# Two residual gates of a diffusion layer: column sums by float32r passes of a high and a low part in place of plain float32 products

## The chip, the cores and the metric

The kernel runs on one NeuronCore of one Trainium2 chip. The metric is the device time of one execution in microseconds, as the median of several runs; shorter is better. One more execution was taken with the profiler; the profile and the trace are of that one.

## The reference

One layer over 1024 latent tokens and 256 context tokens of width 1024, cut to what matters here:

```python
m_lat = silu(c) @ w_mod[l] + b_mod[l]
sh1, sc1, g1, sh2, sc2, g2 = split(m_lat, 6)
h_lat = rms_norm(x, norm1_g) * (1 + sc1) + sh1
y_lat = token_mixers(h_lat, h_ctx, ...)      # retention and differential attention
x = x + g1 * y_lat
h2 = rms_norm(x, norm2_g) * (1 + sc2) + sh2
x = x + g2 * conv_ffn(h2, ...)
return rms_norm(x, final_g)
```

The two residual gates g1 and g2 are rows of 1024 numbers, products of the conditioning vector silu(c) with two 1024 x 1024 blocks of w_mod plus a bias. All inputs and outputs are float32.

## The kernel before

The work runs in stages on one core: the modulation of the first norm and the turned input; the combined input projection in seven column blocks of 512 (blocks 2, 5, 6 for the context, 1, 0, 3, 6, 4), each streamed as four slices of weights; retention beside the last of these blocks; differential attention; the output projection; the gated MLP with a seven-product scheme for the up and the down projection; the final norm.

Nearly all products are made in three float32r passes. An operand is split into a high part, a copy rounded to float32r (ScalarE), and a low part, the difference (VectorE). `passes` (lines 128 to 133) then adds high x high, high x low and low x high into one PSUM tile; its three matmuls are lines 131, 132 and 133 of the profile. A few products are plain float32, whose operands are not split; each of them shows as two matmul records.

The change lies in the stage of the input projection from block 5 to block 0. `transposed` (from line 468) makes one tile of 128 x 512 outputs for each head and half of the tokens: eight k, three passes each, and one `tick()` behind each k. Behind the eighth it calls `rotated` (line 440), which turns the tile: ScalarE copies the swapped quarters or halves (L445, tile xb), VectorE multiplies and adds (L448, L449, L450, tile xa). For the attention's keys `split_store` (line 433) then makes a high part (L436) and a low part (L437) in a tile xhl and stores it (L438). For the queries of the retention `decayed` (line 427) instead lets GpSimd make two scaled copies in a tile xq (L430) and stores them (L431). xhl and xq share one ring of two buffers (tag "xhl" in the pool er). `natural` makes token-major tiles, L411 to L425 its endings. Weights come by `slice_load` (L189) into raw and are split by `split_slice` (L196 the high part, L197 the low part).

Beside this stage runs a generator, `modulations` (from line 490). One `next` of it is made at each tick; the stage has 240 ticks, the generator goes through 233 yields. It has 32 steps of seven yields, eight steps for each of four blocks of w_mod: shift, scale and gate of the second norm, and the gate of the first, in the order g1 (i = 0), two shifts and scales, g2 (i = 3). A step loads a 128 x 1024 piece (L497) and adds it, scaled by the column of silu(c), into an accumulator macc (L511); the accumulators start at zero (L506) with the bias in row 0 (L507). What is left is the sum of macc over the 128 partitions, which `modulated2` makes:

```python
if i in (0, 3):
    dst = g1_d if i == 0 else g2_d
    for n in range(2):
        pg = pst.tile([P, 512], F32, name="pg", tag="tr")
        mm(pg, ones, acc[:, n * 512 : (n + 1) * 512], start=True, stop=True)
        st = ev.tile([P, 512], F32, name="st", bufs=3)
        nc.scalar.copy(st, pg)
        nc.sync.dma_start(out=dst[:, n * 512 : (n + 1) * 512], in_=st)
        yield
```

A 128 x 128 matrix of ones times macc gives the sum in every partition (L528, tile pg); ScalarE copies it out (L530) and it is stored (L531) for the output projection and for the down projection, which read it much later. For i = 1 and 2 the sums are made as columns, by products with two columns of ones (L536). These sums begin one step after their last accumulation for i = 0, 1, 2, and behind the last step for i = 3, where they fall on the last head of block 0.

Where nothing else is said, a planner puts the instructions on the engines: from an estimate of durations it takes, for each engine that is free, the ready instruction that stands first in the source. On each engine the order is then fixed. Other parts of the kernel (the start, attention, the first blocks of the up projection, the end) pin the order of the source on chosen engines by `in_order`; this stage does not. `issue_after` in `modulations` keeps each load and each accumulation behind the newest store and rotation.

The matrix ones (line 112) is also read by `spare`, a few products at the start that only keep TensorE busy (line 655), and by L536.

Of the kernel before, what the change touches and what calls it, by code (L numbers as in the profile page):

```python
# [8 lines left out]
F32 = mybir.dt.float32  # L9
F32R = mybir.dt.float32r  # L10
BF16 = mybir.dt.bfloat16
AF = mybir.ActivationFunctionType
ALU = mybir.AluOpType
# [4 lines left out]
P = 128  # L18
# [51 lines left out]
def r32(ap):  # L70
    return ap.bitcast(F32)
# [3 lines left out]
def kernel(  # L75
# [16 lines left out]
    nc = tc.nc  # L92
    mm = nc.tensor.matmul

    kp = ctx.enter_context(tc.tile_pool(name="kp", bufs=1))
# [13 lines left out]
    nc.sync.dma_start(out=ident, in_=consts[:, K_ID : K_ID + P])  # L109
    mhalf = kp.tile([P, 32], F32, name="mhalf")  # L110
    nc.vector.memset(mhalf, -0.5)
    ones = kp.tile([P, P], F32, name="ones")
    nc.vector.memset(ones, 1.0)

    def rsqrt(out_ap, in_ap, mul, eps, n):
# [39 lines left out]
    with ExitStack() as p1:  # L155
# [334 lines left out]
        def modulations():  # L490
# [11 lines left out]
            for n in range(n_steps):  # L502
                i, k = divmod(n, KD)
                if k == 0:
                    maccs[i] = m2p.tile([P, D], F32, name="macc", bufs=2)
                    nc.gpsimd.memset(maccs[i], 0.0)  # L506
                    nc.sync.dma_start(out=maccs[i][0:1, :], in_=rows[:, R_BMOD + (2 + i) * D : R_BMOD + (3 + i) * D])  # L507
                if n + 2 < n_steps:
                    step_load(n + 2)
                with after("dve"):  # L510
                    nc.vector.scalar_tensor_tensor(out=maccs[i], in0=wms.pop(n), scalar=csil[:, k, 0:1], in1=maccs[i], op0=ALU.mult, op1=ALU.add)  # L511
                for _ in range(MOD_TICKS):
                    if done is not None and k > 0:
                        next(done, None)
                    yield
                if k == KD - 1:
                    done = modulated2(i)
# [4 lines left out]
        def modulated2(i):  # L522
            acc = maccs.pop(i)
            if i in (0, 3):
                dst = g1_d if i == 0 else g2_d
                for n in range(2):
                    pg = pst.tile([P, 512], F32, name="pg", tag="tr")
                    mm(pg, ones, acc[:, n * 512 : (n + 1) * 512], start=True, stop=True)  # L528
                    st = ev.tile([P, 512], F32, name="st", bufs=3)
                    nc.scalar.copy(st, pg)  # L530
                    nc.sync.dma_start(out=dst[:, n * 512 : (n + 1) * 512], in_=st)  # L531
                    yield
            else:
                pg = pst.tile([P, KD, 2], F32, name="pg2", tag="tr")
                for d in range(KD):
                    mm(pg[:, d, :], acc[:, d * P : (d + 1) * P], ones[:, 0:2], start=True, stop=True)  # L536
                    yield
                if i == 1:
                    nc.vector.tensor_copy(m2[:, 0, :], pg[:, :, 0])
                else:  # L540
                    nc.vector.tensor_scalar(out=m2[:, 1, :], in0=pg[:, :, 0], scalar1=1.0, scalar2=None, op0=ALU.add)
                    nc.vector.tensor_tensor(out=m2[:, 1, :], in0=m2[:, 1, :], in1=cl[:, COL_N2 : COL_N2 + KD], op=ALU.mult)
# [4 lines left out]
        with ExitStack() as p0:  # L547
# [121 lines left out]
            start = len(nc.cur_bb.bb.instructions)  # L669
# [49 lines left out]
            part = [pool.tile([P, 512], F32, name="pn", tag="mm") for pool in (ps_a, ps_a, ps_b, ps_b)]  # L719
# [48 lines left out]
        er = p1.enter_context(tc.tile_pool(name="er", bufs=2, reuse_waits="tile"))  # L768
# [26 lines left out]
        with tc.tile_pool(name="rc0", bufs=1) as r0:  # L795
# [20 lines left out]
            acc = r0.tile([P, 8], F32, name="acc")  # L816
# [241 lines left out]
        start = len(nc.cur_bb.bb.instructions)  # L1058
# [59 lines left out]
    with ExitStack() as p2:  # L1118
# [4 lines left out]
        start = len(nc.cur_bb.bb.instructions)  # L1123
        order = sorted(TAU.items(), key=lambda it: it[1] % 1.0)
        for n in range(n_units + 8):
# [6 lines left out]
            if n in (8, 10, 12, 14):  # L1132
                a, i = divmod(n // 2 - 4, 2)
# [210 lines left out]
    with ExitStack() as p4:  # L1344
# [142 lines left out]
        start = len(nc.cur_bb.bb.instructions)  # L1487
# [95 lines left out]
    with ExitStack() as p5:  # L1583
# [43 lines left out]
        acc = [fin.tile([P, D], F32, name=f"acc{t}") for t in range(NT)]  # L1627
# [80 lines left out]
        start = len(nc.cur_bb.bb.instructions)  # L1708
# [130 lines left out]
```

## Time and profile before

| what | us |
|---|---|
| median of 3 runs (lowest to highest) | 1388.44 (1387.87 to 1389.47) |
| the profiled execution | 1388.11 |
| its span, first to last instruction | 1386.3 |
| TensorE busy in it | 1365.4 |
| VectorE, ScalarE, GpSimd busy | 1018.0, 738.6, 346.4 |
| the four gate products (eight records of L528) | first at 136.7, last at 264.1 |

In the lists of the profile PE is TensorE (PEld its weight loads, PEldq the queue of those), DVE VectorE, ACT ScalarE, POOL GpSimd and SP SyncE (SPq its queue of transfers). L528 is line 528 of the kernel. A row of a timeline has the start and the duration in microseconds, the engine, the line, the operation with what it writes and reads, how often it stands there in succession (x2), and in brackets how long the engine had been idle and what ended that; "issue" means that nothing in the trace explains it. A row of a source line or a tile has the durations as lowest, median and highest in nanoseconds. A row of waits has the total, how often, and the longest. A row of transfers ends with the microseconds from issue to landing. A row of windows has the stretch, its length, then for PE, PEld, DVE, ACT and POOL the busy time and the number of instructions, the granted clock of TensorE as a share of the full one, the busy share of the DMA engines and GB/s. Matmuls overlap in the array, so that their durations add up to more than the time that they take; the distance of starts is what they cost.

### The profile page before, as it was taken

The numbers are of one execution on the slowest core, as the hardware profiler recorded it, in microseconds if no ns is written. First come the engines' busy times: TensorE is split into PE (matmuls) and PEld (weight loads), VectorE is DVE, ScalarE is ACT, GpSimd is POOL, SyncE is SP. The second block draws the span as 40 slices with busy tenths as digits, with TensorE's granted clock in tenths as the row PEclk, the third lists the DMA queues.
The fourth block names the chain that finished last, engine by engine and source line by source line (L and its number), as shares of the span: only waits on it lengthen the run. The fifth ranks groups of instructions, "written<-read, shape, count | busy, mean of one in ns | idle before, by whom it ended". The sixth has DMA issues, their size and how long they took to land.

```text
span 1386.3 us, 19666 instructions
## 1 busy us (share of the span) xinstructions
PE 1365.4 (98%) x7028; PEld 1145.9 (83%) x7028; DVE 1018.0 (73%) x1512; ACT 738.6 (53%) x1410; POOL 346.4 (25%) x384
## 2 busy tenths in 40 slices
PE   8999999999999999999999999999999999999997
PEld 6788788888888799998888888888888888888886
DVE  5967866623467898896347998887778877898756
ACT  5536534313466789987037654555545555455533
POOL 1310001501446433411101343222332220043003
PEclk9999999999999999999999999999999999999999
DMA  9467887786678488631221223332323326953334
GB/s 384 153 206 252 295 265 249 254 273 185 191 221 231 133 217 186 140 94 70 106 99 46 92 107 114 114 114 92 114 100 113 111 69 224 393 180 109 122 99 152
DMA packets 107305, 231.14 MB, mean 167 GB/s; under 512 B 9604, under 2 KB 42884, under 8 KB 105288
## 3 DMA queue, kind: packets, MB, share of 16 engines
q1 hardware_dynamic: 98936, 204.73, 43.3%
q0 software_dynamic: 8128, 24.91, 7.9%
q8 instruction: 55, 0.90, 0.3%
q14 instruction: 42, 0.34, 0.1%
q10 hardware_dynamic: 144, 0.26, 0.1%
HBM read 165.37 MB, written 64.23 MB: 166 GB/s over the span
## 4 chain that ended last, share of the span: by engine, by line
PE 65%; DVE 1%; POOL 1%; issue 0%; ACT 0%; DMA 0%; SPq 0%; POOLq 0%; ACTq 0%; DVEq 0%
PE chain L131 6%; PE chain L132 6%; PE chain L133 6%; PE c L132 5%; PE c L133 5%; PE c L131 5%; PE pv L929 5%; PE pA L897 5%; PE third L131 3%; PE third L133 3%; PE third L132 3%; PE pt L917 2%; PE po L133 2%; PE po L132 2%; PE po L131 2%; PE second L131 1%
## 5 line engine op out<-in xcount | busy, mean ns | idle before, releaser
L131 PE MATMUL pl<-hT,whi 128*128 128x512 f32 x256 | 107.6, 420 | 0.0
L131 PE MATMUL chain<-T,whi 128*128 128x512 f32 x264 | 102.8, 389 | 0.0
L132 PE MATMUL chain<-T,whi 128*128 128x512 f32 x264 | 102.7, 389 | 0.0
L133 PE MATMUL chain<-T,wlo 128*128 128x512 f32 x264 | 102.7, 389 | 0.0
L133 PE MATMUL pl<-hT,wlo 128*128 128x512 f32 x256 | 100.4, 392 | 0.0
L132 PE MATMUL pl<-hT,whi 128*128 128x512 f32 x256 | 100.3, 392 | 0.0
L900 DVE TENSOR_REDUCE mt<-pA 128x1 f32<-128x1280 f32 x64 | 95.2, 1490 | 3.8 <-PE pA L897 2.3
L133 PE MATMUL c<-whi,ghl 128*128 128x512 f32 x232 | 90.4, 390 | 0.0
L131 PE MATMUL c<-whi,ghl 128*128 128x512 f32 x232 | 90.3, 389 | 0.0
L132 PE MATMUL c<-wlo,ghl 128*128 128x512 f32 x232 | 90.3, 389 | 0.0
L1310 POOL TENSOR_TENSOR cmb<-wrb 128x512 f32<-128x512 f32 x20 | 30.3, 1517 | 237.6 <-DMA wrb<-w_up 157.3
L897 PE MATMUL pA<-ks,qhl 128*128 128x512 f32 (+1 forms) x384 | 89.6, 368 | 0.0
L904 ACT ACTIVATE p<-pA,mt 128x1280 f32<-128x1280 f32 x64 | 85.5, 1336 | 3.8 <-DVE mt L900 3.4
L131 PE MATMUL pn<-whi,hT 128*128 128x512 f32 x192 | 85.0, 443 | 0.0
L445 ACT ACTIVATE xb<-pl 32x512 f32<-32x512 f32 (+1 forms) x88 | 52.0, 591 | 61.6 <-PE pl L133 41.9
L1161 ACT CAST whi<-cmb 128x512 fp32r<-128x512 f32 x62 | 38.4, 622 | 77.5 <-PE chain L132 64.3
L929 PE MATMUL pv<-va,aT 128*128 128x128 f32 x640 | 77.1, 276 | 0.4 <-DVE yT L958 0.3
L897 PEld LDWEIGHTS pA<-ks,qhl 128*128 128x128 f32 x384 | 67.9, 189 | 11.5
L133 PE MATMUL pn<-whi,hT 128*128 128x512 f32 x192 | 75.8, 396 | 1.0 <-POOL hT L610 1.0
L132 PE MATMUL pn<-wlo,hT 128*128 128x512 f32 x192 | 75.4, 393 | 0.0
L929 PEld LDWEIGHTS pv<-va,aT 128*128 128x128 f32 x640 | 74.0, 192 | 1.2 <-DVE yT L958 0.8
L1162 DVE TENSOR_TENSOR wlo<-cmb,whi 128x512 fp32r<-128x512 f32 x62 | 58.7, 951 | 18.1 <-ACT whi L1161 18.1
(336 smaller groups left out, 3889.7 us busy)
## 6 DMA issues: line engine op xcount, KB each, us to landing
raw<-w_in SPq DMA_DIRECT2D x32, 512.0 KB, 6.0
wm<-w_mod SPq DMA_DIRECT2D x32, 512.0 KB, 4.6
wra<-w_up SPq DMA_DIRECT2D x24, 512.0 KB, 3.3
wrb<-w_up SPq DMA_DIRECT2D x23, 512.0 KB, 3.5
W<-w_down SPq DMA_DIRECT2D x44, 256.0 KB, 6.2
ad<-s SPq DMA_DIRECT2D x20, 512.0 KB, 3.4
wra<-ad SPq DMA_DIRECT2D x20, 512.0 KB, 3.3
wrb<-ad SPq DMA_DIRECT2D x18, 512.0 KB, 4.6
```

The source lines that it names most:

```text
L131: mm(ps, lh, rh, start=first, stop=False, skip_group_check=more)
L132: mm(ps, lh, rl, start=False, stop=False, skip_group_check=more)
L133: mm(ps, ll, rh, start=False, stop=last, skip_group_check=more)
L445: nc.scalar.activation(xb[q * blk : (q + 1) * blk, :], pt[o : o + blk, :], AF.Copy, scale=scale)
L897: mm(self.pa[m][:, c0:c1], self.q[:, i, m, qs], self.k[:, m, c0:c1], start=(i == 0), stop=(i == 1))
L900: nc.vector.tensor_reduce(out=self.mt[:, m : m + 1], in_=self.pa[m][:, :LK], axis=AX.X, op=ALU.min)
L904: nc.scalar.activation(self.p[m], self.pa[m][:, :LK], AF.Exp, scale=-1.0, bias=self.mt[:, m : m + 1], accum_out=self.s[:, m : m + 1])
L917: nc.tensor.transpose(self.pt[g][:, i, :], self.p[0][:, (4 * g + i) * P : (4 * g + i + 1) * P], ident)
L929: mm(self.pv, self.aT[:, c, :], self.v[:, c, :], start=(c == 0), stop=(c == NKT - 1))
L1161: nc.scalar.copy(hi, src)
L1162: nc.vector.tensor_tensor(out=lo, in0=src, in1=r32(hi), op=ALU.subtract)
L1310: nc.gpsimd.tensor_tensor(out=s1, in0=b1, in1=b2, op=ALU.add)
```

## The change

The sums of the two gates are made in two float32r passes. ScalarE makes a high part of each half of macc, VectorE a low part, in a tile of the xhl ring; three yields later two matmuls with ones, one for each part, add into the same PSUM tile. The products of ones with the high and the low part together give the sum to nearly float32's precision. The matrix ones is now allocated as float32r and read as plain float32 by the other uses. `modulated2` has four yields for each half in place of one, so the generator goes through 239 of the stage's 240 ticks.

```diff
-    ones = kp.tile([P, P], F32, name="ones")
+    ones_r = kp.tile([P, P], F32R, name="ones")
+    ones = r32(ones_r)
     nc.vector.memset(ones, 1.0)
...
             if i in (0, 3):
                 dst = g1_d if i == 0 else g2_d
                 for n in range(2):
+                    part = acc[:, n * 512 : (n + 1) * 512]
+                    hl = er.tile([P, 2, 512], F32R, name="xhl")
+                    nc.scalar.copy(hl[:, 0, :], part)
+                    nc.vector.tensor_tensor(out=hl[:, 1, :], in0=part, in1=r32(hl[:, 0, :]), op=ALU.subtract)
+                    for _ in range(3):
+                        yield
                     pg = pst.tile([P, 512], F32, name="pg", tag="tr")
-                    mm(pg, ones, acc[:, n * 512 : (n + 1) * 512], start=True, stop=True)
+                    for a in range(2):
+                        mm(pg, ones_r, hl[:, a, :], start=(a == 0), stop=(a == 1))
                     st = ev.tile([P, 512], F32, name="st", bufs=3)
                     nc.scalar.copy(st, pg)
                     nc.sync.dma_start(out=dst[:, n * 512 : (n + 1) * 512], in_=st)
                     yield
```

## The prediction

> **What bounds the kernel.** I read the page first, then the waits of TensorE over the whole span, then the timeline around the four products of the two gates.
>
> ```profile
> span 1386.3 us, 19666 instructions
> ## 1 busy us (share of the span) xinstructions
> PE 1365.4 (98%) x7028; PEld 1145.9 (83%) x7028; DVE 1018.0 (73%) x1512; ACT 738.6 (53%) x1410; POOL 346.4 (25%) x384
> ...
> PEclk9999999999999999999999999999999999999999
> ```
>
> ```profile
> PE pt L917 <- ACT aT L923: 1.9, 3, 0.7
> ```
>
> TensorE is busy for 1365.4 of 1386.3 us at full clock, and the largest entry in the list of its waits is 1.9 us in three pieces. So a microsecond taken out of TensorE's stream comes off the time, unless a later wait takes it back, and one put into it is paid. This profiled execution took 1388.11 us (1.8 more than its span), the median of the three runs is 1388.44; I sum changes and add them to the median. A difference below 0.2%, 2.8 us, is about what a measurement of this kernel cannot tell from no change.
>
> **What the products cost now.** The timeline of TensorE at the first one, and the rows of its source line:
>
> ```profile
> 136.44 0.40 PE L133 MATMUL pl<-hT,wlo 128*128 128x512 f32 x1
> 136.68 1.02 PE L528 MATMUL pg<-macc,ones 128*128 128x512 f32 x2
> 137.14 0.79 PE L131 MATMUL pl<-hT,whi 128*128 128x512 f32 x1
> 137.77 0.39 PE L132 MATMUL pl<-hT,whi 128*128 128x512 f32 x1
> 138.00 0.39 PE L133 MATMUL pl<-hT,wlo 128*128 128x512 f32 x1
> ```
>
> ```profile
> L528 PE MATMUL pg<-macc,ones x8: 590/592/596, 136.7 to 264.1; 128*128 128x512 f32 x8
> L528 PEldq EVENT_SEMAPHORE  x2: 51/948/1846, 132.6 to 258.1; - x2
> ```
>
> Durations overlap, so cost is read from starts. Neighbouring float32r passes start 0.23 us apart (137.77 to 138.00). From L133 at 136.44 to L132 at 137.77 are 1.33 us; with L131 alone between them it would be two spacings, 0.46. One plain product, two records of 592 ns, thus costs the stream 0.87 us. There are four (eight records). Each becomes two float32r passes of the same shape, 0.46 us, which removes 0.41 us each: **1.64 us in all, 0.12%**. That is the most that the arithmetic itself can give, and it is below what can be measured.
>
> [...]
>
> The last row also shows what a wait of a product does: the weight queue took two semaphore waits, 0.05 and 1.85 us long, the first at 132.6, yet the array did not idle before 136.68, because the queue runs some 4 us ahead. A late operand costs only what it is late by when the array arrives. Queued behind it are the pl passes, which cannot go round it.
>
> **First gate: what is added.** Per half, ScalarE copies the sums to a high part and VectorE subtracts, then three ticks (nine passes) later come the products. So the first pair is due 10 spacings after 136.44, at 138.74. ScalarE and VectorE at that time:
>
> ```profile
> 137.53 0.28 ACT L840 ACTIVATE kd<-kd,lg 128x1 f32<-128x1 f32 x1
> 139.33 0.62 ACT L436 CAST xhl<-xa 128x512 fp32r<-128x512 f32 x1 [1.51 <-issue]
> 139.97 1.20 ACT L445 ACTIVATE xb<-pl 32x512 f32<-32x512 f32 x2
> 141.19 0.59 ACT L530 COPY st<-pg 128x512 f32<-128x512 f32 x1
> ```
>
> ```profile
> 137.23 0.69 DVE L448 SCALAR_TENSOR_TENSOR xa<-pl,rtab 128x512 f32<-128x512 f32 x1 [1.66 <-ACT xb L445]
> 137.84 0.68 DVE L449 TENSOR_TENSOR xb<-xb,rtab 128x512 f32<-128x512 f32 x1
> 138.56 0.69 DVE L450 TENSOR_TENSOR xa<-xa,xb 128x512 f32<-128x512 f32 x1
> 139.17 1.28 DVE L511 SCALAR_TENSOR_TENSOR macc<-wm,csil,macc 128x1024 f32<-128x1024 f32 x1
> 140.36 0.68 DVE L437 TENSOR_TENSOR xhl<-xa,xhl 128x512 fp32r<-128x512 f32 x1
> 140.97 1.28 DVE L511 SCALAR_TENSOR_TENSOR macc<-wm,csil,macc 128x1024 f32<-128x1024 f32 x1
> ```
>
> Two things stand here. The prices: a high part is 0.62 us (L436), a low part 0.68 us (L437), the same shapes and types as the new ones. And a lag: the head that ends on TensorE at 136.44 has its L445 only at 139.97, some 3 us later. The next window's rotation is thus still in VectorE's queue when the array comes for the pair. The high part also needs a buffer of the two-deep xhl ring, whose earlier content must have been stored:
>
> ```profile
> 135.00 0.52 SPq L438 DMA_DIRECT2D dk<-xhl  x1
> ```
>
> ```profile
> dk<-xhl SPq DMA_DIRECT2D x1, 512.0 KB, 3.2
> ```
>
> That store is issued at 135.00 and lands at 138.2, so the high part ends at 138.8 at the earliest, in ScalarE's gap between 137.81 and 139.33. The low part then goes where the planner puts it in VectorE's order: in place of the sum at 139.17 it ends at 139.85, behind L437 at 141.65, behind the second sum (which also precedes it in the source) at 142.9. Against 138.74 the array waits **1.1, 2.9 or 4.2 us**; nothing if the planner moves the pair itself further back. It plans with durations of its own, and the lag shows that VectorE runs later than it planned. I take 2.6, about the middle of 1.1 and 4.2, as no row prefers an end. The second half should find its parts in time: four ticks of 0.69 us and the first pair lie between, and TensorE's wait has used up the lag. Net for this gate at TensorE: 2.6 - 2 x 0.41 = +1.8 us.
>
> What takes some of this back is the one place in this stage where TensorE waits already, for weights of the next two blocks:
>
> ```profile
> PE pn L132 <- DVE wlo L197: 0.5, 2, 0.3
> ```
>
> ```profile
> 152.94 1.22 DVE L197 TENSOR_TENSOR wlo<-raw,whi 128x1024 fp32r<-128x1024 f32 x1
> 154.39 0.69 DVE L448 SCALAR_TENSOR_TENSOR xa<-pl,rtab 128x512 f32<-128x512 f32 x1 [0.23 <-ACT xb L445]
> ```
>
> ```profile
> 154.32 0.65 SPq L189 DMA_DIRECT2D raw<-w_in  x1
> ```
>
> ```profile
> 161.78 1.05 ACT L196 CAST whi<-raw 128x1024 fp32r<-128x1024 f32 x1 [3.66 <-DMA raw<-w_in]
> ```
>
> A TensorE that comes 1.8 us later no longer meets this 0.5: +1.3 us remain. But the same place sets a floor. The load at 154.32 waits for the buffer that L197 at 152.94 frees, and ScalarE at 161.78 waits for that load; VectorE has only 0.23 us of slack beside it. Two low parts put 2 x 0.68 = 1.36 us ahead of it, so the weights come some 1.1 us later, even if the products never waited. The larger of the two holds: **+1.3 us**. On ScalarE the two high parts (1.24 us) mostly fill its gaps; if they don't, they push the same chain by at most as much, which the upper end holds. The SyncE queue gets no new transfer; its two gate stores move back by three ticks or so, with weight loads behind them, and those loads are the ones just priced. In the xhl ring two more tiles go round, so the next head's copy waits for a store one generation younger; that is ScalarE's lag again, off TensorE's path until the place above.
>
> **Second gate.** Here ScalarE and VectorE are not late:
>
> ```profile
> 256.92 1.20 ACT L445 ACTIVATE xb<-pl 64x512 f32<-64x512 f32 x2 [4.29 <-issue]
> 262.41 1.20 ACT L445 ACTIVATE xb<-pl 64x512 f32<-64x512 f32 x2 [4.29 <-issue]
> ```
>
> ```profile
> 263.70 0.69 DVE L448 SCALAR_TENSOR_TENSOR xa<-pl,rtab 128x512 f32<-128x512 f32 x1 [3.47 <-ACT xb L445]
> ```
>
> ```profile
> 258.74 0.36 SPq L431 DMA_DIRECT2D rqk<-xq  x1
> ```
>
> ```profile
> rqk<-xq SPq DMA_DIRECT2D x1, 512.0 KB, 2.8
> ```
>
> ```profile
> 262.16 1.03 PE L528 MATMUL pg<-macc,ones 128*128 128x512 f32 x2
> ```
>
> ScalarE idles 4.29 us and VectorE 3.47 us before the head's rotation. The buffer's store lands at 258.74 + 2.8 = 261.5, so the two parts are made by 262.9, ahead of a pair due three ticks (2.1 us) after 262.16. Later xq tiles on GpSimd wait for a younger store, with no TensorE work near behind them. The idle time hides both parts: **-0.82 us**. Without that cover they would cost up to 0.62 + 0.68 per half.
>
> Ones as float32r: the other uses read it as plain float32, nothing changes there. **Sum: +1.3 - 0.8 = +0.5 us, 1388.9 us.** With the bounds: stall 1.1 gives 1.1 - 0.82 - 0.5 - 0.82 = -1.0; stall 4.2 gives +2.1. The forecast's own range is 1387.4 to 1390.5.
>
> **Rivals.** *Clean gain.* The planner lets the pair stand further back or the low part earlier, and the weights are not pushed: -1.64, **1386.8**. For it: 73% busy VectorE has room on average. Against it: the 3 us lag and the 0.23 us of slack.
>
> *The array's clock drops.* The end of the span shows what an idle array does:
>
> ```profile
> 1377.67 0.39 PE L133 MATMUL c<-W,wlo 128*128 128x512 f32 x1
> ```
>
> ```profile
> 1381.00:1382.00 1.00, 0.00 (x0) 0.00 (x0) 0.74 (x1) 0.72 (x1) 0.23 (x1) 1.00 0.20 74
> 1382.00:1383.00 1.00, 0.00 (x0) 0.00 (x0) 0.01 (x1) 0.00 (x0) 0.00 (x0) 0.75 1.02 373
> ```
>
> The last matmul ends at 1378.06; the granted clock is 1.00 to 1382 and 0.75 over the next microsecond, a fall to half at about 1382.5, 4.4 us of idleness. The stall's upper bound, 4.2, almost reaches that. If it passes 4.4 us, the passes behind it run at half rate; estimated as long as the fall took, 4.4 us, they lose 2.2 us. With the +2.1 of the upper bound this is +4.3, **1392.7**: slower. [...]
>
> *The change doesn't do what it says:* eight float32r passes run at plain cost, 4 x 0.87 = +3.5 us, 1391.9. The starts 0.23 us apart of L131 to L133, which read the same type, speak against it.
>
> **Chances.** Forecast 0.53; clean gain 0.25; clock drop 0.15; plain cost 0.02; the rest, 0.05, to a new order of the planner's behind this stage that gains more than the arithmetic. Only that rest passes -2.8 us: faster 0.05. Of the drop most, and the plain cost, pass +2.8: slower 0.13. Same 0.82. The range reaches from the clean gain less 0.4 of scatter, 1386.4, to the forecast's upper end with 1.0 of scatter, 1391.5.
>
> **What would show it.** Right: pairs of L131-like records 0.23 us apart instead of the 1.02 us records; TensorE waiting 1 to 4 us for a low part near 139, none near 264; the L132 wait near 164 gone or alike. Wrong: no wait near 139 (then the clean gain, if the weights are on time), a clock below 1.00 near 143, waits on the second gate's low part, or a different order of heads later.

## The result, and the profile after

The changed kernel took 1395.98 us in the median of six runs (1394.26 to 1398.91), the kernel before 1388.74 (1387.87 to 1389.96). The ratio is 1.0056, with a 95% interval of 1.0046 to 1.0066: **7.2 us slower**. The forecast was 1388.9 with a range to 1391.5. The profiled execution of the changed kernel took 1395.24 us, with a span of 1393.5, against 1386.3 before.

The page of the profile after, and the list of TensorE's waits over the span:

```profile
span 1393.5 us, 19676 instructions
## 1 busy us (share of the span) xinstructions
PE 1364.7 (98%) x7028; PEld 1145.6 (82%) x7028; DVE 1020.9 (73%) x1516; ACT 741.0 (53%) x1414; POOL 348.4 (25%) x384
...
PEclk9999999999999999999999999999999999999999
```

```profile
PE pub L351 <- DMA kvgb<-kvg: 2.4, 1, 2.4
PE px L634 <- DVE sm L117: 2.3, 2, 1.9
PE pt L925 <- ACT aT L931: 1.9, 3, 0.7
PE pg L536 <- DVE xhl L531: 1.6, 1, 1.6
PE third L132 <- DVE ub L1441: 1.6, 1, 1.6
PE pt L1209 <- DVE x L1204: 1.5, 2, 1.1
...
PE pc L280 <- DMA qk<-rqk: 1.1, 1, 1.1
```

Numbers of lines between L112 and L526 have grown by one, those behind the changed lines by eight. TensorE's busy time hardly changed (1364.7 against 1365.4); its idle time within the span grew from 20.9 to 28.8 us. New in the list are pub for kvgb, pg for a low part, pt (L1209) and pc (px is a wait at the start, and 2.8 us in a second profile of the kernel before). The wait of third had 0.7 us before.

**The first gate.** The timelines of TensorE, VectorE and ScalarE:

```profile
138.04 0.40 PE L134 MATMUL pl<-hT,wlo 128*128 128x512 f32 x1
138.93 0.50 PE L536 MATMUL pg<-xhl,ones 128*128 128x512 f32 x1 [0.49 <-ACT xhl L530]
139.27 0.40 PE L132 MATMUL pl<-hT,whi 128*128 128x512 f32 x1
141.31 0.80 PE L536 MATMUL pg<-xhl,ones 128*128 128x512 f32 x1 [1.65 <-DVE xhl L531]
141.90 0.63 PE L133 MATMUL pl<-hT,whi 128*128 128x512 f32 x1
142.33 0.63 PE L134 MATMUL pl<-hT,wlo 128*128 128x512 f32 x1
```

```profile
138.78 0.68 DVE L438 TENSOR_TENSOR xhl<-xa,xhl 128x512 fp32r<-128x512 f32 x1
139.38 1.28 DVE L512 SCALAR_TENSOR_TENSOR macc<-wm,csil,macc 128x1024 f32<-128x1024 f32 x1
140.57 0.69 DVE L531 TENSOR_TENSOR xhl<-macc,xhl 128x512 fp32r<-128x512 f32 x1
```

```profile
138.27 0.61 ACT L530 CAST xhl<-macc 128x512 fp32r<-128x512 f32 x1
```

The high part ended at 138.88, close to the 138.8 of the forecast. The low part stands behind the second sum (L512), the last of the three places that the forecast named, and ends at 141.26. From L134 at 138.04 to the high pass are 0.89 us, 0.66 more than a spacing of 0.23; from L132 at 139.27 to the low pass are 2.04, 1.81 more: 2.5 us of waiting in all. Then the passes start 0.43 us apart. The windows tell why (the number behind POOL's is the granted clock):

```profile
138.00:142.00 4.00, 1.86 (x6) 0.89 (x6) 3.93 (x6) 3.23 (x6) 0.00 (x0) 0.89 0.35 123
142.00:146.00 4.00, 4.00 (x14) 3.18 (x13) 2.85 (x6) 1.72 (x3) 0.56 (x1) 0.68 0.94 291
```

The clock fell to half, in the trace's record of granted clocks for 3.413 us, from 141.12 to 144.54. Eight spacings of starts, from 141.31 to 144.74, take 3.43 us in place of 8 x 0.23 = 1.84: some 1.6 us are lost.

**The second gate.** SyncE's queue, first before, then after:

```profile
264.24 1.47 SPq L531 DMA_DIRECT2D g2d<-st  x2
...
269.41 0.37 SPq L431 DMA_DIRECT2D rqk<-xq  x1
269.83 2.71 SPq L231 DMA_DIRECT2D kvgb<-kvg  x5
```

```profile
272.87 0.37 SPq L432 DMA_DIRECT2D rqk<-xq  x1
273.33 0.46 SPq L539 DMA_DIRECT2D g2d<-st  x1
273.84 1.80 SPq L232 DMA_DIRECT2D kvgb<-kvg  x3
```

The kvgb loads, first operands of the next stage's heads, are queued behind the store of an xq tile, now also behind the second gate store. They are issued 4.0 us later, 1.6 of which TensorE itself is late by there. TensorE, after:

```profile
278.28 0.49 PE L351 MATMUL pub<-kvgb 128*128 128x128 f32 x2 [2.35 <-DMA kvgb<-kvg]
```

The xq tile is late from three places, one on each engine:

```profile
263.95 0.62 ACT L530 CAST xhl<-macc 128x512 fp32r<-128x512 f32 x1 [4.26 <-DMA rqk<-xq]
264.60 1.20 ACT L446 ACTIVATE xb<-pl 64x512 f32<-64x512 f32 x2
```

```profile
267.04 1.22 DVE L198 TENSOR_TENSOR wlo<-raw,whi 128x1024 fp32r<-128x1024 f32 x1
268.17 0.69 DVE L451 TENSOR_TENSOR xa<-xa,xb 128x512 f32<-128x512 f32 x1
```

```profile
268.99 3.85 POOL L431 TENSOR_TENSOR xq<-xa,qd 128x512 f32<-128x512 f32 x2 [4.03 <-DVE xa L451]
```

The high part waits for the buffer and stands ahead of the rotation's copies (264.60 against 262.41 before). The planner has put the split of a weight slice (L198) ahead of the rotation's last step (268.17 against 265.03), and GpSimd starts at 268.99 in place of 265.86.

### The profile page after: what moved, and what is told of

Same layout as the page of the kernel before. It is cut to its first block, busy times and chain, and to the rows that moved or that the text cites. A ratio compares the mean times of both kernels' runs of the same rounds, so it can differ in the third digit from the quotient of the medians.

```text
span 1393.5 us, 19676 instructions
## 1 busy us (share of the span) xinstructions
PE 1364.7 (98%) x7028; PEld 1145.6 (82%) x7028; DVE 1020.9 (73%) x1516; ACT 741.0 (53%) x1414; POOL 348.4 (25%) x384
## 4 chain that ended last, share of the span: by engine, by line
PE 62%; DVE 3%; issue 1%; DMA 1%; POOL 1%; ACT 0%; SPq 0%; POOLq 0%; DVEq 0%; ACTq 0%
PE chain L133 5%; PE chain L134 5%; PE chain L132 5%; PE c L133 5%; PE c L134 5%; PE c L132 5%; PE pv L937 5%; PE pA L905 5%; PE third L132 3%; PE third L134 3%; PE third L133 3%; PE pt L925 2%; PE po L134 2%; PE po L133 2%; PE po L132 2%; PE second L133 1%
## 5 line engine op out<-in xcount | busy, mean ns | idle before, releaser
L132 PE MATMUL pl<-hT,whi 128*128 128x512 f32 x256 | 106.5, 416 | 0.0
L132 PE MATMUL chain<-T,whi 128*128 128x512 f32 x264 | 102.8, 389 | 0.0
L134 PE MATMUL chain<-T,wlo 128*128 128x512 f32 x264 | 102.7, 389 | 0.0
L134 PE MATMUL pl<-hT,wlo 128*128 128x512 f32 x256 | 100.9, 394 | 0.0
L132 PE MATMUL c<-whi,ghl 128*128 128x512 f32 x232 | 90.2, 389 | 0.0
L134 PE MATMUL c<-whi,ghl 128*128 128x512 f32 x232 | 90.2, 389 | 0.0
L132 PE MATMUL pn<-whi,hT 128*128 128x512 f32 x192 | 85.0, 443 | 0.0
L134 PE MATMUL pn<-whi,hT 128*128 128x512 f32 x192 | 75.9, 396 | 1.0 <-POOL hT L618 1.0
L1169 ACT CAST whi<-wra 128x512 fp32r<-128x512 f32 x55 | 34.0, 621 | 69.1 <-PE third L133 43.5
```

The source lines that it names most:

```text
L132: mm(ps, lh, rh, start=first, stop=False, skip_group_check=more)
L134: mm(ps, ll, rh, start=False, stop=last, skip_group_check=more)
L1169: nc.scalar.copy(hi, src)
```

## The experiments

Theory: the cost is two waits of TensorE, one at each gate, and stretches at half clock behind them. Rivals: a slowing spread over the kernel; the second gate alone; the later order alone, without the parts. Diffs are against the changed kernel. Each set ran beside the kernel before on its own chip; its median there is given.

**The same kernel again.**

> The changed kernel itself once more, for its spread and for a second trace. Theory A (three places: the wait for the low part of the first gate with the clock drop behind it, about +2.2 us once the weights' wait is over; the kvgb loads behind a late store after the second gate, +2.5 less 0.8; and waits far behind at 441, 750 and 825 us, +3.9 together): 5 to 9 us over before, with the first two places as in the first trace. If the three late waits belong to the change they come again at the same instructions; if they are scatter of the transfers they do not, and the median stays below the sum of all places. Rival B (a uniformly slower kernel, by other orders of work everywhere): TensorE's shift grows evenly, not in steps.

1394.93, ratio 1.0050 (1.0037 to 1.0062; before 1388.32). The waits at both gates recur, and this profile has two stretches of 3.4 us at half clock, one behind each (0.996 of the clock was granted over the span, 0.99 from 276 to 280 and 0.58 from 280 to 284). Laid beside the kernel before, instruction by instruction, TensorE's stream is shifted in a few steps and is level between them: no uniform slowing. At the first gate TensorE waits 3.6 us here (1.75 and 1.81), against 2.5 in the first profile. Of the late waits those of third and pt come again, that of pc does not.

**One gate alone** (the other with its plain product and without yields; the diff is of the first gate alone, the second has i == 3).

```diff
+                    if i == 0:
                         part = acc[:, n * 512 : (n + 1) * 512]
...
+                    else:
+                        pg = pst.tile([P, 512], F32, name="pg", tag="tr")
+                        mm(pg, ones, acc[:, n * 512 : (n + 1) * 512], start=True, stop=True)
```

> Only the first gate in two float32r passes, the second as before. Theory A: the wait near 139 us and the half clock behind it for 3.4 us, the kvgb wait gone; 2 to 3 us over before, 4 to 6 if the late waits follow from any shift. Rival C (the second gate's store order carries nearly all of the loss): within 1 us of before.

> Only the second gate in two float32r passes, the first as before. Theory A: clock 1.00 throughout, products cheaper by 0.8 us, the kvgb wait of 2 to 2.5 us near 277; 1 to 2 us over before, 3 to 5 if the late waits follow from any shift. Rival C: 4 to 7 us over before.

First gate alone 1393.48, 1.0037 (1.0023 to 1.0051); second alone 1392.95, 1.0034 (1.0021 to 1.0046). Either gate costs; the second does not carry it alone. The sum of the two, 9.8 us, is above the 6.6 of both together on that chip; with the repetition of the first gate alone further down (3.4 us) it is 8.0. Whether the two share part of their cost is therefore not shown.

**The order alone**: plain products, 3 yields ahead of each, no parts; run twice.

```diff
-                    part = acc[:, n * 512 : (n + 1) * 512]
-                    hl = er.tile([P, 2, 512], F32R, name="xhl")
-                    nc.scalar.copy(hl[:, 0, :], part)
-                    nc.vector.tensor_tensor(out=hl[:, 1, :], in0=part, in1=r32(hl[:, 0, :]), op=ALU.subtract)
                     for _ in range(3):
                         yield
                     pg = pst.tile([P, 512], F32, name="pg", tag="tr")
-                    for a in range(2):
-                        mm(pg, ones_r, hl[:, a, :], start=(a == 0), stop=(a == 1))
+                    mm(pg, ones, acc[:, n * 512 : (n + 1) * 512], start=True, stop=True)
```

> Plain products and no parts, only the three yields ahead of each product, so that the planner's order of stores, loads and weight parts changes nearly as in the changed kernel. Theory A: within 1 us of before, as the copies and subtractions and the ring of buffers are what comes late. Rival D (the later place of the products and the new order of SyncE's queue cost it): 4 to 7 us over before, with the kvgb wait near 275 us.

> The kernel with plain products 3 yields later, once more: it had 1390.3 in the median though its profiled execution (1388.45) showed no new wait. If the 2 us are of the order of the work, the median is again 1389.5 to 1391 and a second profile shows where (a wait, or a stretch at half clock of 3.4 us); if they were the chip of that day, 1388.0 to 1389.

1390.33, 1.0012 (1.0003 to 1.0021), and 1390.12, 1.0010 (1.0001 to 1.0019). Some 1.6 to 2.0 us belong to the later place and the planner's new order, more than the 1 us that the theory allowed. No wait over 0.2 us at either gate; the second profile has a wait of pt (L1203) of 1.1 us that the first has not, for the same program. Where the rest of these 2 us goes the profiles do not show.

**The second gate's parts in another ring.**

```diff
-                    hl = er.tile([P, 2, 512], F32R, name="xhl")
+                    hl = (er.tile([P, 2, 512], F32R, name="xhl") if i == 0 else m2p.tile([P, 2, 512], F32R, name="ghl", tag="wm2", bufs=3))
```

> Changed kernel, but the parts of the second gate lie in the ring of the weights of the sums (wm2), which nothing else uses any more by then, and no longer in the xhl ring. Kept theory (two waits of TensorE, each of which may bring a stretch of 3.4 us at half clock): the second gate's copy of the high part no longer waits for the store of an xq tile, the xq tile of L446 is not held up, its store comes no later than in the kernel before, and pub (L351) does not wait for kvgb: the time is that of the kernel with the new form at the first gate alone, 1393.5, or up to 0.8 less: 1392.5 to 1394. Rival (the two parts' work on ScalarE and VectorE costs the time, wherever they lie): 1395 as the changed kernel.

**The first pair later.**

```diff
-                    for _ in range(3):
+                    for _ in range(6 if i == 0 and n == 0 else 3):
                         yield
```

> Changed kernel, but the first pair of passes of the first gate stands 3 ticks further behind its parts (6 in place of 3), which is ten products of 0.23 us or 2.3 us. Kept theory (wait for the low part behind the second half of the sum on VectorE, then a stretch at half clock): the wait at 139 us shrinks from 1.65 to under 0.5 us and no half-clock stretch follows there; the second gate keeps its wait for kvgb: the time is that of the kernel with the new form at the second gate alone, 1393.0, within 0.8: 1392.2 to 1393.8. Rival (the parts' work itself): 1395, whatever the passes' place.

**Both edits.**

> Both edits: second gate's parts in the other ring, first gate's first pair 3 ticks later. Kept theory: both waits are gone, what is left is the passes' gain of up to 1.6 us and what the later order alone gave (the kernel with plain products 3 ticks later stood at 1390.3): 1387.5 to 1390.5, the kernel before being at 1388.3. Rival (the parts' work itself): 1395, as the changed kernel.

1393.20 (1.0041, 1.0028 to 1.0053), 1395.22 (1.0050, 1.0038 to 1.0063) and 1395.49 (1.0051, 1.0039 to 1.0064); before 1388.6. The edits did not remove the waits that they were aimed at. In the other ring the high part no longer waits for a store, yet pub still waits for kvgb; VectorE's and GpSimd's rows of that kernel:

```profile
PE pub L351 <- DMA kvgb<-kvg: 1.9, 1, 1.9
```

```profile
266.77 1.21 DVE L198 TENSOR_TENSOR wlo<-raw,whi 128x1024 fp32r<-128x1024 f32 x1
267.91 0.68 DVE L451 TENSOR_TENSOR xa<-xa,xb 128x512 f32<-128x512 f32 x1
```

```profile
268.72 3.53 POOL L431 TENSOR_TENSOR xq<-xa,qd 128x512 f32<-128x512 f32 x2 [2.42 <-issue]
```

The split still stands ahead of the rotation's last step and the xq tile is as late: the ring alone is not the cause. Three more yields for the first pair, in turn, only moved the waits: the low pass waits 1.5 us at 142.3, and the second half's passes, which had none, now 0.7 and 1.0 us.

**The parts made but not read**, plain products in the same places.

```diff
-                    for a in range(2):
-                        mm(pg, ones_r, hl[:, a, :], start=(a == 0), stop=(a == 1))
+                    mm(pg, ones, acc[:, n * 512 : (n + 1) * 512], start=True, stop=True)
```

> Changed kernel, but the sums are done by plain float32 products straight from the sums; both parts are still made in the xhl ring and nothing reads them. Kept theory: no wait for the low part at the first gate (the product needs only the sum), so no cost there; the second gate's ring wait and the wait for kvgb stay: the time is that of the kernel with the new form at the second gate alone plus up to 0.8 for its plain products: 1392 to 1394. Rival 1 (the parts' work itself): 1395 plus the plain products' 1.6, or 1396 to 1397. Rival 2 (only the two passes and their order cost time): 1390.3 as with plain products 3 ticks later.

1391.12, 1.0017 (1.0008 to 1.0026; before 1388.6): 0.8 to 1.0 above the order alone, and 0.9 below the least that the theory gave. No wait at the first gate; pub waits 1.7 us for kvgb, so parts and order delay those loads whatever reads the parts. But most of the 6 to 7 us needs passes that read the parts.

**Early parts.** Right behind the last sum of a block, one step ahead of their products. At the second gate both halves lie in the idle ring of the sums' weights and the passes stand where the plain products stood, with no yields; at the first gate only the first half is early. `make(n)` makes the two parts of half n. The diff, cut, has both gates.

```diff
                 if k == KD - 1:
                     done = modulated2(i)
+                    if i in (0, 3):
+                        next(done)
...
+                hls = [make(n) for n in range(1 if i == 0 else 2)]
+                yield
                 for n in range(2):
+                    if i == 0 and n == 1:
+                        hls.append(make(n))
+                        for _ in range(3):
+                            yield
```

> New form at the first gate alone, plain products at the second. The two parts of the first half stand right behind the last sum of the block, ahead of the first sum of the next block, one step before their passes, which stand where the plain product stood; the parts of the second half stand behind the first pair, with the 3 yields. Kept theory (the passes wait because the low part stands behind a sum on VectorE): no wait for a part at 139 us, no half-clock stretch there, against the 1.7 and 1.4 us of the kernel with the new form at the first gate alone: 1387.0 to 1390.0, against its 1393.5 and the 1388.4 of the kernel before. Rival (the parts' work itself on ScalarE and VectorE): 1393.5 stays.

> New form at the second gate alone, plain products at the first. The parts of both halves stand right behind the last sum, in the ring of the weights of the sums, and the passes where the plain products stood, with no yields added. Kept theory (the parts' work, and the split of a weight slice that moves ahead of the rotation's last step, push the xq tile on GpSimd, its store, and the kvgb loads behind it on SyncE): no wait of pub for kvgb at 274 us, against the 2.6 us of the kernel with the new form at the second gate alone: 1387.0 to 1389.5, against its 1393.0 and the 1388.4 of the kernel before. Rival (the ring wait or the parts' place do not matter, any part work beside this head delays the loads): the wait stays over 1 us and the time at 1391 to 1393.

> Both edits: the new form at both gates, with its parts early. Kept theory: neither wait, four products of 0.87 us replaced by four pairs of 0.46: 1386.5 to 1390.0, the kernel before being at 1388.4; this is the version that could beat both. Rival (the parts' work itself): 1395, as the changed kernel.

Second gate 1389.55, 1.0008 (0.9999 to 1.0016); first 1392.19, 1.0023 (1.0015 to 1.0032); both 1393.42, 1.0034 (1.0022 to 1.0047); before 1388.55. At the second gate the cost is gone, 3.4 us under the same form with 3 yields, and pub no longer waits for kvgb. SyncE and TensorE there:

```profile
263.93 1.89 SPq L554 DMA_DIRECT2D g2d<-st  x2
...
269.58 0.37 SPq L432 DMA_DIRECT2D rqk<-xq  x1
270.05 2.18 SPq L232 DMA_DIRECT2D kvgb<-kvg  x4
```

```profile
272.71 0.38 PE L351 MATMUL pub<-kvgb 128*128 128x128 f32 x2
```

But a later pub waits for another operand, Sb, which VectorE makes behind a weight split; before, that split started at 280.01:

```profile
281.51 1.23 DVE L198 TENSOR_TENSOR wlo<-raw,whi 128x1024 fp32r<-128x1024 f32 x1 [3.90 <-ACT whi L197]
```

```profile
283.05 0.49 PE L351 MATMUL pub<-kvgb 128*128 128x128 f32 x2 [0.98 <-DVE Sb L245]
```

So TensorE gains 0.8 us at the second gate's passes, as forecast, and loses 1.0 here, a wait that neither profile of the kernel before has. In the new order the load of these weights stands later in SyncE's queue (274.00 against 272.65), and their high part, which waits for it, is started at 280.43 in place of 278.92.

At the first gate the planner left the early high part behind the copy of the next head. ScalarE and TensorE:

```profile
138.37 0.62 ACT L437 CAST xhl<-xa 128x512 fp32r<-128x512 f32 x1 [1.51 <-issue]
138.89 0.61 ACT L533 CAST xhl<-macc 128x512 fp32r<-128x512 f32 x1
```

```profile
139.56 0.50 PE L549 MATMUL pg<-xhl,ones 128*128 128x512 f32 x1 [2.61 <-ACT xhl L533]
```

The pass is due earlier and its part is not: TensorE waits 2.6 us in one piece (3.4 in the kernel with both gates early), and half clock follows it: from 140.63 to 142.77 the passes of the first gate's early parts start 0.43 us apart.

**Far passes.** At the first gate 12 yields between parts and passes; once with plain products at the second gate, once with its early parts.

```diff
-                    for _ in range(3):
+                    for _ in range(12):
                         yield
```

> New form at the first gate alone, parts made where the changed kernel makes them, passes 12 yields behind them in place of 3 for both halves; plain products at the second gate. Kept theory (the cost of the first gate is TensorE's wait for parts that VectorE and ScalarE, a head behind TensorE there, make too late, and the half-clock stretch that such a wait can bring): no wait for a part, no half-clock stretch, 1387.0 to 1390.5. Rival (moving the parts' work onto these two engines delays the rotations and the weights behind them): 1391 to 1393.5, the kernel with 3 yields having 1393.5 and the one with early parts 1392.2, with a wait for weights or a rotation in place of the wait for the part.

> Both gates in the new form: the first with its passes 12 yields behind the parts, the second with both halves' parts right behind the last sum in the other ring and no added yields. Kept theory: neither wait is left, 1386.5 to 1390.0; the version that could beat both. Rival: 1391 to 1395.

1389.00, 1.0005 (0.9996 to 1.0014), and 1389.62, 1.0012 (1.0003 to 1.0021); before 1388.47. No pass waits for a part any more, pub does not wait for kvgb, and with distance alone the first gate's cost is gone. TensorE and VectorE at the first gate, far passes:

```profile
144.13 0.39 PE L134 MATMUL pl<-hT,wlo 128*128 128x512 f32 x1
144.36 0.62 PE L537 MATMUL pg<-xhl,ones 128*128 128x512 f32 x2
144.82 0.39 PE L132 MATMUL pl<-hT,whi 128*128 128x512 f32 x1
```

```profile
139.49 1.28 DVE L512 SCALAR_TENSOR_TENSOR macc<-wm,csil,macc 128x1024 f32<-128x1024 f32 x1
140.68 0.69 DVE L532 TENSOR_TENSOR xhl<-macc,xhl 128x512 fp32r<-128x512 f32 x1
```

The low part is as late as ever, 141.37, behind the same sum; its pass now comes at 144.6. So at the first gate the wait costs, not the parts' work. A pair takes 0.69 - 0.23 = 0.46 us, as forecast. Yet no version beats the kernel before. With both gates mended TensorE's stream is 2.3 us ahead of the second profile of the kernel before at 275 us; pub's wait for Sb (0.9 us) leaves 1.2 at 283, and a wait of pt (L1221) of 1.1 us near 750 takes the rest. Nor is all of the 2.3 the passes' gain: early parts at the second gate, with plain products at the first, are ahead by as much.

**The kernel before again.**

> The kernel before, run as one of these. Median 1388.0 to 1389.0, within 0.1 per cent of the other runs of it. Its second profile tells whose the late waits are: third near 825 (0.7 us in the first profile, 1.6 in every changed one) and pt near 750 (none in the first, 0.9 to 1.5 in most changed ones). If they are the scatter of executions, this profile shows 1.6 and 1.1 too; if they come from the changes, it shows 0.7 and none.

1388.63, ratio 1.0000 (0.9991 to 1.0009). Of its second profile:

```profile
PE third L131 <- DVE ub L1433: 1.6, 1, 1.6
```

The longer wait of third is thus scatter of executions, no work of the change. A wait of pt near 750 is in neither profile of the kernel before, and in eleven of the seventeen profiles of changed ones (0.9 to 1.5 us; a twelfth has 0.7 us near 727). The order alone has it in one of its two profiles, so scatter has a part in it; whether the change has one too is open.

**The wait filled, and the first gate alone again.**

```diff
+                        for _ in range(6 if n == 0 else 0):
+                            mm(pg, ones_r, hl[:, 0, :], start=True, stop=True)
                         for a in range(2):
```

> The kernel with the new form at the first gate alone and 3 yields, with six extra passes of ones and the high part of the first half ahead of its pair (their result is overwritten by the pair's first pass). They stand in the 1.7 us in which TensorE waits for the low part, so they need no time of their own (6 x 0.23 = 1.4 us), but leave TensorE idle for 0.5 us there in place of 1.7. If stretches at half clock that follow the wait carry part of the first gate's cost (1.7 us in every execution that has one): 1391.0 to 1392.4, no half clock in the profile near 140. If the wait alone carries it: as the same kernel without the extra passes, 1393.0 to 1394.0 (1393.5 in its first five runs), or up to 0.4 more.

> The kernel with the new form at the first gate alone, once more, for the comparison on one chip: median 1392.5 to 1394.0. Its first profile had no stretch at half clock and the lowest time of its five runs (1391.4). If the half clock comes and goes by where the wait falls in the 3.413 us windows of the clock record, this profile has one near 140 and a time near 1393, or none and a time near 1391.4.

Filled 1392.16, 1.0030 (1.0019 to 1.0041); again 1391.92, 1.0026 (1.0016 to 1.0035); before 1388.54. The second profile of the first gate alone does have the half clock that the first had not, in the windows:

```profile
138.00:142.00 4.00, 1.76 (x8) 0.81 (x6) 3.93 (x6) 3.49 (x6) 0.00 (x0) 1.00 0.24 93
142.00:146.00 4.00, 4.00 (x11) 3.14 (x12) 3.23 (x5) 1.73 (x3) 0.00 (x0) 0.57 1.00 272
```

The filled kernel has none (1.00 from 134 to 146) and is no faster. Its passes stand in another order and TensorE loses 1 us near 724 as well, so it does not decide what the half clock costs. The granted clock of the single timed executions gives an estimate: its mean, short of the kernel before's and times the span, is the time lost, if TensorE would have been busy throughout. The changed kernel has 0.9962 in the mean of its six executions against 0.9981 to 0.9984 for the kernel before beside the experiments: some 2.6 to 3 us. Its repetition has 0.9968 against 0.9982 (2.0 us), the second gate alone the same (2.0), the first alone 0.9978 and 0.9974 against 0.9982 and 0.9981 (0.6 and 1.1), early parts at the first gate, alone or with the second, 0.9970 against 0.9984 (2.0), the second gate's parts in the other ring 1.2, the first pair later 0.7, both 0.9, the filled kernel and early parts at the second gate 0.2 or less. Each value is recorded to 0.001, and the mean also counts the stretch at half clock behind the last matmul (3.1 us of the span in the profile after, 3.8 in the one before), which costs nothing; the values of the changed kernel lie between 0.993 and 0.998. So the estimates are good to about 1 us for the kernels with five or six executions, and to some 0.4 us for those with eleven.

## Why the prediction was wrong

*What a product and a pair cost.* Right: a pair takes 0.46 us, and at the second gate's passes, where nothing waits, the stream gains the 0.8 us that was forecast.

*First gate, the wait.* Right in mechanism; that the size agrees, 2.5 us in the profile where 2.6 was taken as a middle value, is luck. The low part stood in the last of the three places, for which 4.2 was reckoned, but VectorE was 1.6 us ahead of the trace before (second sum at 139.38 against 140.97). It was so already two heads earlier, ahead of any part. The rows are of the kernel before, of the changed one, and of the changed one again:

```profile
131.07 0.69 DVE L448 SCALAR_TENSOR_TENSOR xa<-pl,rtab 128x512 f32<-128x512 f32 x1 [2.13 <-ACT xb L445]
129.48 0.69 DVE L449 SCALAR_TENSOR_TENSOR xa<-pl,rtab 128x512 f32<-128x512 f32 x1 [2.13 <-ACT xb L446]
130.96 0.69 DVE L449 SCALAR_TENSOR_TENSOR xa<-pl,rtab 128x512 f32<-128x512 f32 x1 [2.12 <-ACT xb L446]
```

The same program thus has this lead in one execution and not in another; without it TensorE waited 3.6 us, and 2.5 to 3.6 in the five profiles with three yields here. The second half found its parts in time, as forecast.

*First gate, what takes it back.* In size too small: 0.5 was granted. Against the second profile of the kernel before TensorE is 3.1 us later at 147.3 and 1.4 later at 167.7, so 1.7 came back; that profile lists 1.0 us of waits for weights there. The floor below it, weights 1.1 us later whatever the products do, did not show: with far passes TensorE leaves this place 1.2 to 1.5 us ahead of the kernel before, though by its lead of that execution VectorE is ahead there too.

*First gate, the clock.* This step failed: the forecast put nothing for it, because only "If it passes 4.4 us" was the drop to come, with a chance of 0.15. It came after 2.5 us of waiting, with passes in between, in some executions and not in all. The rival had the right kind of loss and waited for too long an idleness; it reckoned 4.4 us at half rate, and the record has 3.413. The 4.4 us read at the end of the span are, in steps of 3.413 us from the first entry of the clock record, the last 1.02 us of one step and one whole; the forecast took their sum for the idleness that a drop needs.

*Second gate.* This step failed outright: "Later xq tiles on GpSimd wait for a younger store, with no TensorE work near behind them. The idle time hides both parts: -0.82". There is such work: pub, whose kvgb loads stand on SyncE behind that tile's store. In place of falling by 0.82, TensorE's lag behind the second profile of the kernel before falls by 0.7 at the passes and then grows by 2.6 at pub, from 1.4 at 167.7 to 3.3 at 278.3. The idle time of ScalarE and VectorE was there, but the high part could start only when the buffer was free, and that was when the rotation was due. The experiments show that the parts' place and the order carry this, and not the ring alone. Whether the late gate store between the xq store and the kvgb loads adds to it was not tried by itself.

*Order later.* "A different order of heads" did not come; the order behind the stage is the same. But waits came: pc for qk<-rqk at 445 (in this profile 1.1 us, and 0.4 in one other) and pt at 751 and 756. They carry the lag from 3.2 to 4.1 and on to 6.0 us; the spans differ by 1393.5 - 1387.6 = 5.9. These two were not forecast, and their cause stays open.

*The sum.* +0.5 was forecast. The medians give +7.2: about 2 to 3 us in half clock, the rest in waits at the two gates and behind, less the passes' gain. In the two profiles of the changed kernel TensorE lags the second profile of the kernel before by 3.3 and 5.9 us at 283 us, behind both gates, and by 5.9 and 7.3 at the end; what comes between is the part without a shown cause.

## What to carry to other kernels

On an engine that is 98% busy, replacing one of its instructions by a cheaper one that needs two others to work first trades a fixed price for a deadline: follow the new operands to the end of the queue in which they stand, and leave a distance greater than those engines' lag, since here 12 ticks in place of 3 were worth 3 to 4.5 us with no other edit. Where idle time of another engine is to hide work, check that the work can start when that idle time begins, and follow whatever the work pushes through the stores and loads behind it to the next wait of the busy engine. A gain of 0.1% isn't worth such a risk: even with both of these waits gone it was not seen, as the next one, for Sb, took back the second gate's part.

## What the runs showed of the hardware

In the trace of the changed kernel the record of granted clocks has half rate from 141.12 us on, for 3.413 us. That is 136.53 us behind the record's first entry, 40.00 times 3.413. The half rate at the end of the span begins at 1390.40 us, 406.04 times 3.413 behind the first entry; in the kernel before it begins at 1382.49 us, 403.04 times.

In steps of 3.413 us from the first entry, TensorE of the changed kernel idled 1.95 us in the step ahead of the half rate at the first gate. It idled 1.73 us in a step at the second gate (274.24 to 277.66) and 1.64 us in one that ends at 834.03, and both were followed by full rate. At the end of the span a step with 1.80 us of idleness was followed by full rate, and the wholly idle one behind it by half rate; in the kernel before these two steps have 1.02 and 3.41 us.

The waits in other profiles of the first gate:

| profile | waits of TensorE, us | behind them |
|---|---|---|
| first gate alone | 1.37 and 1.66 | passes 0.23 us apart |
| first gate alone, again | 0.59 and 1.65 | 0.57 of the clock granted from 142 to 146 |
| the wait filled | 0.84 and 0.49 | 1.00 from 142 to 146 |
| early parts at the first gate | 2.61 in one piece | passes 0.43 us apart |

At the second gate the changed kernel's wait of 2.35 us left the clock at 1.00 from 270 to 282, and the same program's 2.0 us, in its repetition, had 0.58 behind it. So the same program has the drop in one execution and not in another, and the longer wait is not always the one that brings it. That a wait may lie in one such step or be cut by two would fit this; it is the author's estimate from the steps above. The idle times come from records of matmuls with modelled ends, and how much idleness brings the drop is not shown.
